# A hybrid attention block on one core: another order of the filler work, preloaded gate weights, byte masks, and a margin in the planner

## The chip, the core and the metric

The kernel runs on one core of a Trainium2 chip. A core has five engines that work side by side, each through its own queue in order: TensorE (PE, matrix products into PSUM), VectorE (DVE), ScalarE (ACT), GpSimd (POOL) and SyncE (SP), which here issues nearly all DMA transfers. The metric is the device time of one execution in microseconds (us); lower is better.

## What is computed

One layer of a hybrid decoder block over 1024 positions and 16 meta tokens in front of them, width 1024, float32. One projection feeds two branches: differential attention (8 heads) and gated linear attention, GLA (4 heads).

```python
u = rms_norm(h, norm_w); proj = u @ w_in
(a_q, a_k, a_v, a_z, g_q, g_k, g_v, g_z, g_lr, gate_a, gate_b) = jnp.split(proj, ...)
q1, q2 = partial_rope(qa[0], pos), partial_rope(qa[1], pos)   # the first 16 of 64 dims are turned
k1, k2 = partial_rope(ka[0], pos), partial_rope(ka[1], pos)
o_a = diff_attention(q1, q2, k1, k2, va, pos, lam)   # softmax(q1 k1) - lam softmax(q2 k2), times v
y_a = (norm(o_a) * silu(a_z)) @ w_branch_a
gk = (g_lr @ gla_gate_w2 + gla_gate_b)
lg = (jax.nn.log_sigmoid(gk) / GLA_GATE_NORMALIZER)
o_b = rms_norm(gla(qb, kb, vb, lg), gla_norm_w)      # chunked scan with decays exp(cumsum(lg))
y_b = (o_b * silu(g_z)) @ w_branch_b
merged = jax.nn.sigmoid(gate_a) * y_a + jax.nn.sigmoid(gate_b) * y_b
return h + merged @ w_out                            # then a final rms_norm; the meta tokens are dropped
```

## The kernel before

Every float32 product is made of three TensorE products of operands split into a high and a low part: `u_hi` with `w_hi`, `u_lo` with `w_hi`, `u_hi` with `w_lo`. ACT makes the high part, VectorE the low one. The kernel runs in stages:

- The front (0 to about 82 us) loads the x tiles, squares and scales them, transposes them on TensorE (L746) and projects the GLA keys.
- The projections (to about 591 us) are Strassen products (L563). They leave the gates in HBM (`d_g`, from tile `sg`, L295), and `ahead()` runs near their end: it loads, through POOL's queue, the first two weight tiles of the next stage.
- The GLA stage (about 592 to 880 us) runs 4 heads in two halves each. A half makes its gates (`ps_g`, L1294; then `lg`, L1303, and scans), the decay of the meta tokens (`dm`, L1344 to L1364, transposed on TensorE by L1348), the state (`st`), and a ladder of levels: `xl` on POOL (L1434), ACT (L1475) and VectorE (L1439), then `ps_l` on TensorE (L1446), then a masked copy (L1450). At its end the output is scaled (`oc`, L1537), transposed (L1542), made into `ob` (L1547) and stored to `d_ob`.
- Beside the heads run the fillers: projections that TensorE can do at any time. `fillers()` lists them in their order. `plain` projects a tile of 128 key columns in three pieces of 346, 348 and 346 positions (24 matmuls each), and `put` evacuates a piece: ACT writes the high part (L1160), VectorE the low part (L1163), SP stores it to `d_k` or `d_q`. `rope` does the same for the two tiles whose positions are turned: ACT copies both tiles to `rr` (L1194), SP loads a cosine and a sine table to `cs` (L1211, L1212), VectorE turns them (four products L1223 and two sums L1225 for a piece), and `put` follows. The rotary key tiles use `rope(8, ...)`; `rope(0, d_q, ...)` does the queries, whose raw projection is read back from HBM.
- Differential attention (about 880 to 1236 us) begins with the scores `ps_s` (L1734), a maximum (L1763) and the softmax on ACT (`p`, L1775); the branch product of GLA, `ps_y`, is its filler. The out stage follows.

Within each stage the order is made by a planner when the program is built (class `Schedule`). An instruction is an `op` with an engine, an estimated duration, dependencies, a priority and the ring (a set of buffers) that it takes a place in. `enter` gives it the earliest time at which its inputs are there: the end of each dependency plus a latency (`LAT`, or `SAME` on the same engine; 2.2 us after a DMA on SP). `run` then takes, engine by engine, the instruction that can start first; those that can start within `AHEAD` of each other go by priority. The result is a fixed order on each engine. On the chip, a semaphore wait holds its engine's whole queue.

Pieces of keys go to ring `qks`, two places which are the key tiles `kk0` and `kk1` of the later attention; `rr` and `cs` have one place each, the query tiles `q0` and `q1`. `PREP` is the time that the planner allows for the first operations of the GLA stage. The gate weights `w2r` (128 partitions, 16 rows of weights and a row of bias in groups of 32) are put together by a POOL memset and six DMAs (L1088 to L1092), and turned into `w2p` and `w2h` by ACT (L1093, L1095) and VectorE (L1096). The level masks come as float32 (`maskr`, L1099) and are cast to bytes on VectorE (L1100).

Of the kernel before, what the change touches and what calls it, by code (L numbers as in the profile page):

```python
# [77 lines left out]
class Schedule:  # L78
# [24 lines left out]
    def run(self):  # L103
# [60 lines left out]
def tile_hybrid_block(  # L164
# [11 lines left out]
    gate_b,  # L176
# [484 lines left out]
    with ExitStack() as es:  # L661
# [15 lines left out]
        def x_tile(i):  # L677
# [25 lines left out]
            ld = op("SP", 1.46 if n == P else 0.3, load, take="xt", lat=2.2, prio=pr)  # L703
# [118 lines left out]
        def keep(dst, lo_t, scale):  # L822
            def evac(_, o, y, ps, t0, n):
                v = {}

                def copy():
                    v["t"] = fe0.tile([P, 512], F32, name="stg", tag="st", bufs=2)[:, :n]
                    act(v["t"], ps(), AF.Copy, scale=scale)

                a = op("ACT", n / 1400 + 0.11, copy, (o,), take="st", use=(y,), prio=-1)  # L830
                op("SP", n / 700, lambda: nc.sync.dma_start(dst[:, t0 - lo_t : t0 - lo_t + n], v["t"]), (a,),
                   use=(("st", a),), lat=2.2, prio=-1)

            return evac
# [167 lines left out]
        b = op("SP", 3.0, begin, rest, lat=2.2, prio=200)  # L1002
# [6 lines left out]
    first = []  # L1009

    def ahead():

        for i in range(2):
            raw = wp["pool"].tile([P, KC * P], F32, name="w_raw", tag="w_raw", bufs=wp["nr"])
            nc.gpsimd.dma_start(raw, w_col[8 + i] if NV else w_row[4, i])
# [4 lines left out]
            first.append(hl)  # L1020

# [8 lines left out]
    def da_v(jobs, g, pre=None):  # L1030
# [3 lines left out]
        def evac(ti, o, y, ps):  # L1034
# [20 lines left out]
            stores.append(op("SP", 0.72, store, (b,), use=(("vs", a),), lat=2.2, prio=-1))  # L1055
# [16 lines left out]
    with ExitStack() as es:  # L1072
# [80 lines left out]
        def put(base, dst, i, raw, use, deps, c, n, t=None):  # L1153
# [16 lines left out]
            a = op("ACT", n / 1400 + 0.11, hi, deps, take="" if t else "qks", use=use, prio=-1)  # L1170
            b = op("DVE+" if t else "DVE", n / 960 + 0.07, lo, (a,), use=use, prio=-1)
            own = t.own if t else ("qks", a)
            qk_ops.append(op("SP", n / 350, store, (b,), use=(own,), lat=2.2, prio=-1))

        kn = [0]
# [6 lines left out]
        def plain(base, dst, i, pieces, lo_t):  # L1182
            w = jobs.weights(w_col[base + i])
            jobs.cols([w], pieces,
                      lambda _, o, y, ps, t0, n: put(base, dst, i, ps, (y,), (o,), slice(t0 - lo_t, t0 - lo_t + n), n))
# [88 lines left out]
        def gla_head(h):  # L1274
# [95 lines left out]
            def half_ops(hf, st):  # L1370
# [209 lines left out]
                for vh in range(2):  # L1580
# [4 lines left out]
                    op("SP", 1.46, lambda vh=vh: obs(vh), (c,), use=(("ob", b), ("oh", a)), lat=2.2, prio=-1)  # L1585
# [7 lines left out]
        def fillers():  # L1593
# [69 lines left out]
    with ExitStack() as es:  # L1663
# [19 lines left out]
        def load_k(h):  # L1683
# [4 lines left out]
            loads["k", h] = op("SP", 3.0 if h > 1 else 0.0, run if h > 1 else lambda: None, take="kk", lat=2.2, prio=16 * h)  # L1688

        def load_q(h, hf):  # L1690
# [4 lines left out]
            loads["q", h, hf] = op("SP", 3.0 if h else 0.0, run if h else lambda: None, take=f"q{hf}", lat=2.2,  # L1695
                                   prio=16 * h + 8 * hf)

        def load_v(h):
            for i, (k, us) in enumerate((("va", 1.5), ("vb", 1.5), ("vm", 0.5))):
                run = (lambda i=i: load_vp(h, i)) if h else lambda: None  # L1700
                st = tuple(vst[h // 2]) if h // 2 >= VA else ()
                loads[k, h] = op("SP", us if h else 0.0, run, st, take=k, lat=2.2, prio=16 * h + (8 if i == 1 else 4))
# [242 lines left out]
        def value(n):  # L1945
# [27 lines left out]
            z = op("SP", 0.5, lambda: load_z(n), (pv,), take="za", lat=2.2, prio=t0)  # L1973
# [27 lines left out]
        def o_load(kind, src, k, prio, deps, cs=(0,)):  # L2001
# [8 lines left out]
            for c in cs:  # L2010
                ops.append(op("SP", 3.0 / len(cs), lambda c=c: run(c), deps[c] + tuple(ops), take="" if c else f"o{k}", lat=2.2,
# [194 lines left out]
        def w_load(kk, late, i, r, deps):  # L2206
# [18 lines left out]
            return op("SP", 1.5 if i == 0 or not late else 0.75, run, deps, take="" if place else "raw" if late else f"wr{i}", lat=2.2, prio=LP)  # L2225

        for kk in range(4):
# [17 lines left out]
            def store(name, kk=kk, t=t, ops=ops):  # L2245
# [3 lines left out]
                stored[name, kk] = op("SP", 0.75, run, (ops[name],), use=(("x4", ops[name]),), lat=2.2, prio=-1)  # L2249
# [37 lines left out]
        def out_pair(p):  # L2287
# [84 lines left out]
            def x_load(i, c):  # L2372
# [6 lines left out]
                ld[i, c] = op("SP", 0.75, run, (s4op,) + d, take="x4" if i == c else "g4", prio=1500 + p, lat=2.2)  # L2379
# [110 lines left out]
def _consts():  # L2490
# [6 lines left out]
    m = np.zeros((P, len(LEVELS), P), f)  # L2497
# [17 lines left out]
def _layout(i):  # L2515
# [4 lines left out]
    hj = lambda m: m.reshape(D, HJ, 8, 8).transpose(0, 2, 1, 3).reshape(D, 1024)  # L2520
    cols = lambda m: m.reshape(KC, P, -1, P).transpose(2, 1, 0, 3)
# [11 lines left out]
        "gate_w2": a["gla_gate_w2"][0],  # L2533
        "gate_b": a["gla_gate_b"],
# [26 lines left out]
```

## Time and profile before

| | |
|---|---|
| median of 3 runs | 1393.76 us (1391.72 to 1394.04) |
| profiled execution | 1394.19 us, its span 1392.4 us |
| TensorE busy | 1332.8 us, 96% of the span |
| VectorE, ScalarE, GpSimd busy | 872.6, 749.0 and 580.9 us |
| mean granted TensorE clock | 0.992 of full speed |

Busy time is the time in which an engine executes, queued waits not counted. An idle time in brackets stands before the instruction that ended it, with what released it. The granted clock is a mean over a stretch; TensorE's two levels are 1.2 and 2.4 GHz, so 0.5 and 1.0.

### The profile page before, as it was taken

The numbers are of one execution on the slowest core, as the hardware profiler recorded it, in microseconds if no ns is written. First come the engines' busy times: TensorE is split into PE (matmuls) and PEld (weight loads), VectorE is DVE, ScalarE is ACT, GpSimd is POOL, SyncE is SP. The second block draws the span as 40 slices with busy tenths as digits, with TensorE's granted clock in tenths as the row PEclk, the third lists the DMA queues.
The fourth block names the chain that finished last, engine by engine and source line by source line (L and its number), as shares of the span: only waits on it lengthen the run. The fifth ranks groups of instructions, "written<-read, shape, count | busy, mean of one in ns | idle before, by whom it ended". The sixth has DMA issues, their size and how long they took to land. (4 is left out here: it accounts for less than half of the span.)

```text
span 1392.4 us, 22201 instructions
## 1 busy us (share of the span) xinstructions
PE 1332.8 (96%) x7736; PEld 1160.0 (83%) x7736; DVE 872.6 (63%) x1457; ACT 749.0 (54%) x1639; POOL 580.9 (42%) x598
## 2 busy tenths in 40 slices
PE   6999999999999999988999989799999999999998
PEld 5988889899888888788998989688888788778776
DVE  4845464555655444447676867487867778557775
ACT  7543332553656656544655454487777777422343
POOL 3113242442444232213463436256575665334444
PEclk9999999999999999999999999999999999999999
DMA  6216373324333333385524473588866555588332
GB/s 218 88 65 204 130 248 120 102 84 137 123 114 121 105 104 116 114 266 154 186 83 151 137 262 114 194 261 266 293 204 204 171 198 155 182 315 273 127 119 86
DMA packets 133747, 229.49 MB, mean 165 GB/s; under 512 B 14322, under 2 KB 60594, under 8 KB 133636
## 3 DMA queue, kind: packets, MB, share of 16 engines
q1 hardware_dynamic: 133348, 227.03, 49.7%
q8 instruction: 61, 1.00, 0.3%
q0 software_dynamic: 288, 1.05, 0.3%
q14 instruction: 50, 0.41, 0.1%
HBM read 143.81 MB, written 84.21 MB: 164 GB/s over the span
## 5 line engine op out<-in xcount | busy, mean ns | idle before, releaser
L511 POOL TENSOR_TENSOR s<-w_raw 128x512 f32<-128x512 f32 x48 | 69.9, 1475 | 194.5 <-DMA w_raw<-in_w_col_dram 133.1
L563 PE MATMUL ps_st<-th,wh 128*128 128x512 f32 x352 | 137.0, 389 | 0.2 <-DVE u L577 0.2
L563 PE MATMUL ps_st<-th,wl 128*128 128x512 f32 x352 | 136.9, 389 | 0.0
L563 PE MATMUL ps_st<-tl,wh 128*128 128x512 f32 x352 | 136.9, 389 | 0.0
L1434 POOL TENSOR_TENSOR xl<-lg 128x256 f32<-128x256 f32 x112 | 78.8, 728 | 93.5 <-PE ps_l L1446 36.8
L246 DVE TENSOR_TENSOR wl<-s,wh 128x512 fp32r<-128x512 f32 x96 | 77.0, 802 | 63.9 <-ACT wh L245 63.9
L245 ACT CAST wh<-s 128x512 fp32r<-128x512 f32 x96 | 59.4, 619 | 102.7 <-PE ps_st L563 56.0
L1775 ACT ACTIVATE p<-ps_s,nm 128x272 f32<-128x272 f32 (+7 forms) x128 | 96.6, 757 | 27.7 <-DVE nm L1763 18.2
L1763 DVE TENSOR_REDUCE nm<-ps_s 128x1 f32<-128x272 f32 (+7 forms) x128 | 97.1, 767 | 21.9 <-PE ps_s L1737 18.5
L426 PE MATMUL ps_proj<-u_hi,w_hi 128*128 128x346 f32 (+3 forms) x320 | 105.5, 330 | 4.7 <-ACT rr L1194 2.2
L563 PE MATMUL ps_st<-u_hi,wh 128*128 128x512 f32 x264 | 102.8, 389 | 1.0 <-issue 1.0
L563 PE MATMUL ps_st<-u_lo,wh 128*128 128x512 f32 x264 | 102.7, 389 | 0.0
L563 PE MATMUL ps_st<-u_hi,wl 128*128 128x512 f32 x264 | 102.7, 389 | 0.0
L427 PE MATMUL ps_proj<-u_lo,w_hi 128*128 128x346 f32 (+3 forms) x320 | 99.7, 312 | 1.3 <-DVE u_lo L755 1.3
L428 PE MATMUL ps_proj<-u_hi,w_lo 128*128 128x346 f32 (+3 forms) x320 | 99.2, 310 | 0.0
L245 ACT CAST wh<-w_raw 128x512 fp32r<-128x512 f32 x70 | 43.1, 616 | 93.5 <-PE ps_st L563 87.9
L246 DVE TENSOR_TENSOR wl<-w_raw,wh 128x512 fp32r<-128x512 f32 x70 | 61.2, 874 | 46.7 <-ACT wh L245 46.7
L563 PEld LDWEIGHTS ps_st<-th,wh 128*128 128x128 f32 x352 | 66.1, 188 | 14.3 <-ACT sg L289 0.6
L1734 PE MATMUL ps_s<-kk,q 128*128 128x264 f32 (+7 forms) x208 | 74.4, 362 | 3.7 <-ACT p L1775 3.6
L563 PEld LDWEIGHTS ps_st<-th,wl 128*128 128x128 f32 x352 | 66.1, 188 | 13.7
L563 PEld LDWEIGHTS ps_st<-tl,wh 128*128 128x128 f32 x352 | 66.1, 188 | 13.7
L511 POOL TENSOR_TENSOR s<-w_raw,s 128x512 f32<-128x512 f32 x22 | 28.5, 1295 | 115.3 <-DVE wl L246 115.3
(401 smaller groups left out, 4307.9 us busy)
## 6 DMA issues: line engine op xcount, KB each, us to landing
w_raw<-in_w_col_dram SPq DMA_DIRECT2D x54, 512.0 KB, 3.7
q<-d_q SPq DMA_DIRECT2D x32, 512.0 KB, 5.3
kk<-d_k SPq DMA_DIRECT2D x16, 520.0 KB, 7.0
d_g<-sg SPq DMA_DIRECT2D x32, 256.0 KB, 2.0
va<-d_v SPq DMA_DIRECT2D x16, 512.0 KB, 5.2
d_q<-qhi SPq DMA_DIRECT2D x24, 256.0 KB, 3.0
d_q<-qlo SPq DMA_DIRECT2D x24, 256.0 KB, 3.4
w_raw<-in_w_row_dram SPq DMA_DIRECT2D x12, 512.0 KB, 3.8
```

Of the source, the lines that this page charges most:

```text
L245: nc.scalar.copy(hi, raw)
L246: (eng or nc.vector).tensor_tensor(lo, raw, hi.bitcast(F32), ALU.subtract)
L426: mm(b["ps"], wh, rh, start=kc == 0, stop=False)
L427: mm(b["ps"], wh, rl, start=False, stop=False)
L428: mm(b["ps"], wl, rh, start=False, stop=kc == KC - 1)
L511: nc.gpsimd.tensor_tensor(r, x, y, op)
L563: mm(ps, w[:, k], x[k], start=start and k == 0 and i == 0, stop=k == KC // 2 - 1 and i == 2, skip_group_check=not start,)
L1434: nc.gpsimd.tensor_tensor(ap(X["xl", li], o1, *to), x if e else ref, ref if e else x, ALU.subtract)
L1734: mm(pp, qh, kk[:, c0 : c0 + w], start=True, stop=False)
L1763: nc.vector.tensor_reduce(b, ps, AX.XY if len(ps.shape) == 3 else AX.X, ALU.max, negate=True)
L1775: act(dst, ps, AF.Exp, bias=b, accum_out=stat[t]["sm"][:, j : j + 1])
```

## The change

- `fillers()`: the plain key tiles 2 and 3 come first, the rotary key tiles third. `ahead()` preloads the weights of those two plain tiles instead of the rotary ones.
- The gate weights are laid out on the host as one array of 128 rows; `ahead()` loads it with one DMA on POOL's queue, into a place of the weight ring. The memset and the six DMAs go.
- The masks are bytes in HBM and are loaded as such; the float32 tile and its cast go.
- Pieces of plain key tiles take their places in turn from `qks`, `qks`, `rr` and `cs`, so from four tiles instead of two.
- The planner: `PREP` is 7 instead of 11; the latency after a DMA is 3.0 instead of 2.2; an instruction on TensorE is taken to be ready 0.5 us (`MARGIN`) after its inputs from other engines. This holds in all stages.

```diff
-PREP = 11.0
-LAT = {"PE": 0.2, "ACT": 0.2, "DVE": 0.2, "POOL": 0.2, "SP": 2.2}
-SAME = {"PE": 0.0, "ACT": 0.13, "DVE": 0.13, "POOL": 0.13, "SP": 2.2}
+PREP = 7.0
+LAT = {"PE": 0.2, "ACT": 0.2, "DVE": 0.2, "POOL": 0.2, "SP": 3.0}
+SAME = {"PE": 0.0, "ACT": 0.13, "DVE": 0.13, "POOL": 0.13, "SP": 3.0}
+MARGIN = 0.5
...
         def enter(o):
-            o.at = max([d.end + (SAME[d.eng] if d.eng == o.eng else d.lat) for d in o.deps], default=0.0)
+            m = MARGIN if o.eng == "PE" else 0.0
+            o.at = max([d.end + (SAME[d.eng] if d.eng == o.eng else d.lat + m) for d in o.deps], default=0.0)
...
-            nc.gpsimd.dma_start(raw, w_col[8 + i] if NV else w_row[4, i])
+            nc.gpsimd.dma_start(raw, w_col[10 + i] if NV else w_row[4, i])
...
+        w2r.append(wp["pool"].tile([P, KC * P], F32, name="w2r", tag="w_hi", bufs=wp["nb"])[:, :512])
+        nc.gpsimd.dma_start(w2r[0], gate_w2)
...
-        w2r = s2.tile([P, 512], F32, name="w2r", tag="gq", bufs=3)
-        nc.gpsimd.memset(w2r, 0.0)
-        for i in range(4):
-            nc.sync.dma_start(w2r[32 * i : 32 * i + 16], gate_w2)
-            if i % 2 == 0:
-                nc.sync.dma_start(w2r[32 * i + 16 : 32 * i + 17], gate_b)
...
-        maskr = s2.tile([P, len(LEVELS), P], F32, name="maskr", tag="gk", bufs=2)
-        nc.sync.dma_start(maskr, c_masks)
-        nc.vector.tensor_copy(masks, maskr)
+        nc.sync.dma_start(masks, c_masks)
...
+            ring = "qks"
+            if not t:
+                ring = ("qks", "qks", "rr", "cs")[pn[0] % 4]
+                pn[0] += 1
+
             def hi():
-                v["t"] = t() if t else qks()
+                v["t"] = t() if t else qks() if ring == "qks" else sq.tile(
+                    [P, 2, 512], F32R, name="qks", tag={"rr": "q0", "cs": "q1"}[ring])
...
-            rope(8, d_k, KP, 0, first if NV else (None, None))
-            plain(8, d_k, 2, KP, 0)
+            for i in (2, 3):
+                plain(8, d_k, i, KP, 0, first[i - 2] if NV else None)
+            rope(8, d_k, KP, 0)
             if not NV:
                 gla_v(1)
-            for i in (3, 4, 5):
+            for i in (4, 5):
                 plain(8, d_k, i, KP, 0)
```

On VectorE, at the start of the GLA stage, this is the order before: the gate weights, the masks, the first turned piece and then the first gate.

```order
411 L1096 TENSOR_TENSOR w2p<-w2r,w2h 64x512
412 L1100 CAST masks<-maskr 128x1024
413 L1223 TENSOR_TENSOR qks<-rr,cs 128x346 x4
414 L1225 TENSOR_TENSOR qks<-qks 128x346 x2
415 L1163 SCALAR_TENSOR_TENSOR qks<-qks 128x346
416 L393 TENSOR_TENSOR w_lo<-w_raw,w_hi 128x512
417 L1163 SCALAR_TENSOR_TENSOR qks<-qks 128x346
418 L1303 SCALAR_TENSOR_TENSOR lg<-ps_g,lgt 128x16
```

And after the change:

```order
410 L1094 TENSOR_TENSOR w2p<-w2r,w2h 64x512
411 L1166 SCALAR_TENSOR_TENSOR qks<-ps_proj,qks 128x346
412 L1166 SCALAR_TENSOR_TENSOR qks<-ps_proj,qks 128x348
413 L1306 SCALAR_TENSOR_TENSOR lg<-ps_g,lgt 128x16
414 L1326 SCALAR_TENSOR_TENSOR lg<-ones,lg 128x16
415 L1347 TENSOR_TENSOR dm<-lg 128x16
416 L1306 SCALAR_TENSOR_TENSOR lg<-ps_g,lgt 128x512
417 L1367 TENSOR_TENSOR dm<-dm,gk 128x16
```

The turns have left this place, and `dm` follows the first gate at once. Their first row now is 482, among the levels of head 0 and behind its first outputs:

```order
481 L1453 COPY_PREDICATED mx_5655<-masks,ps_l 128x256 x3
482 L1226 TENSOR_TENSOR qks<-rr,cs 128x348 x4
483 L1228 TENSOR_TENSOR qks<-qks 128x348 x2
484 L1550 SCALAR_TENSOR_TENSOR ob<-ps_t,glaw,gz 128x512
485 L1166 SCALAR_TENSOR_TENSOR qks<-qks 128x348 x2
```

On SP at the start of the stage the last gate store (`d_g`) stood ahead of the masks before:

```order
136 L1090 DMA w2r<-in_gate_w_dram 16x512
137 L1092 DMA w2r<-in_gate_b_dram 1x512
138 L1090 DMA w2r<-in_gate_w_dram 16x512
139 L295 DMA d_g<-sg 128x512
140 L1090 DMA w2r<-in_gate_w_dram 16x512
141 L1092 DMA w2r<-in_gate_b_dram 1x512
142 L1090 DMA w2r<-in_gate_w_dram 16x512
143 L1099 DMA maskr<-in_c_masks_dram 128x1024
```

After the change it stands behind them:

```order
136 L1096 DMA masks<-in_c_masks_dram 128x1024
137 L1098 DMA ones<-in_c_ones_dram 128x128
138 L1100 DMA tri<-in_c_tri_dram 128x256
139 L1259 DMA gk<-d_gk 128x16
140 L1254 DMA gk<-d_gk 128x2x128
141 L296 DMA d_g<-sg 128x512
142 L1254 DMA gk<-d_gk 128x2x128 x3
```

The six loads of the gate weights are gone, and the gate store is now the sixth issue of the stage. On TensorE, the transpose of `dm` stands at row 3233 before, behind two gates (`ps_g`) and 189 filler matmuls of the stage, and at row 3115 after, behind 72. At the end of the GLA stage its last eight transposes and the first branch products stood next to each other before:

```order
4427 L453 MATMUL ps_proj<-w_hi,u_lo 128x256
4428 L454 MATMUL ps_proj<-w_lo,u_hi 128x256
4429 L1542 MATMUL ps_t<-ident,oc 128x128 x8
4430 L447 MATMUL ps_y<-w_hi,u_hi 48x256
4431 L448 MATMUL ps_y<-w_lo,u_hi 48x256
```

After the change the eight are two groups with 9 filler matmuls between them, and 30 of the kind that begins here stand behind the second group, before the first `ps_y` at row 4434:

```order
4401 L454 MATMUL ps_proj<-w_hi,u_lo 128x256
4402 L455 MATMUL ps_proj<-w_lo,u_hi 128x256
4403 L1545 MATMUL ps_t<-ident,oc 128x128 x4
4404 L453 MATMUL ps_proj<-w_hi,u_hi 128x256
4405 L454 MATMUL ps_proj<-w_hi,u_lo 128x256
4406 L455 MATMUL ps_proj<-w_lo,u_hi 128x256
```

Fillers have moved from earlier in the stage to its end.

## Rows read from the trace of the kernel before

**Rows 1.** The page: span, and busy time, share and instructions of each engine.
```profile
span 1392.4 us, 22201 instructions
PE 1332.8 (96%) x7736; PEld 1160.0 (83%) x7736; DVE 872.6 (63%) x1457; ACT 749.0 (54%) x1639; POOL 580.9 (42%) x598
```

**Rows 2.** Windows by stage: width, busy us of each engine, granted clock, DMA share, GB/s.
```profile
0.00:50.00 50.00, 35.47 (x248) 33.09 (x249) 30.76 (x56) 34.77 (x65) 14.44 (x25) 1.00 0.49 163
592.00:660.00 68.00, 59.09 (x342) 56.16 (x343) 43.96 (x96) 31.00 (x70) 17.08 (x23) 0.92 0.71 215
660.00:800.00 140.00, 136.23 (x930) 128.16 (x930) 103.04 (x214) 76.82 (x194) 66.67 (x80) 1.00 0.45 137
800.00:880.00 80.00, 72.61 (x521) 67.26 (x520) 52.55 (x109) 40.59 (x106) 33.21 (x39) 0.98 0.54 173
880.00:905.00 25.00, 19.17 (x122) 16.78 (x123) 12.31 (x25) 10.85 (x30) 9.20 (x14) 0.86 0.72 246
905.00:1236.00 331.00, 324.21 (x2076) 273.90 (x2075) 236.37 (x420) 230.15 (x608) 191.72 (x235) 1.00 0.67 221
```

**Rows 3.** Timeline of PE, GLA start: start, duration, instruction, idle before and releaser.
```profile
609.63 0.50 PE L1294 MATMUL ps_g<-glp,w2p 128*128 128x512 f32 x1 [1.80 <-DVE lg L1303]
620.85 0.43 PE L426 MATMUL ps_proj<-u_hi,w_hi 128*128 128x346 f32 x1 [2.24 <-ACT rr L1194]
633.21 0.38 PE L1348 MATMUL ps_t<-ident,dm 128*16 128x128 f32 x1 [3.36 <-DVE dm L1364]
```

**Rows 4.** Timeline of DVE at the GLA start: turns, gate, dm.
```profile
604.03 1.81 DVE L1223 TENSOR_TENSOR qks<-rr,cs 128x346 f32<-128x346 f32 x4 [1.02 <-DMA cs<-in_c_sin_dram]
...
616.41 0.52 DVE L1223 TENSOR_TENSOR qks<-rr,cs 128x348 f32<-128x348 f32 x1 [4.20 <-DMA d_k<-qks]
...
619.85 0.68 DVE L1303 SCALAR_TENSOR_TENSOR lg<-ps_g,lgt 128x512 f32<-128x512 f32 x1
...
627.68 0.52 DVE L1223 TENSOR_TENSOR qks<-rr,cs 128x346 f32<-128x346 f32 x1 [2.34 <-DMA d_k<-qks]
...
632.99 0.17 DVE L1364 TENSOR_TENSOR dm<-dm,gk 128x16 f32<-128x16 f32 x1
```

**Rows 5.** Timeline of ACT: the first evacuation of the GLA stage.
```profile
599.73 0.45 ACT L1194 COPY rr<-ps_proj 128x346 f32<-128x346 f32 x1 [3.82 <-DMA d_g<-sg]
```

**Rows 6.** Timeline of SP's queue: last gate store and masks.
```profile
595.94 0.35 SPq L295 DMA_DIRECT2D d_g<-sg  x1
...
598.81 0.35 SPq L1099 DMA_DIRECT2D maskr<-in_c_masks_dram  x1
```

**Rows 7.** Timelines of ACT and PE, 811 to 817 us.
```profile
811.91 1.23 ACT L1160 ACTIVATE qks<-qks 128x512 fp32r<-128x512 f32 x2 [3.15 <-DVE qks L1225]
...
814.69 0.33 PE L1542 MATMUL ps_t<-ident,oc 128*128 128x128 f32 x1 [2.29 <-ACT oc L1537]
815.85 1.21 PE L1542 MATMUL ps_t<-ident,oc 128*128 128x128 f32 x3 [0.83 <-ACT oc L1537]
```

**Rows 8.** Timeline of POOL; then L1439 by line: ns min/median/max.
```profile
623.23 4.35 POOL L1434 TENSOR_TENSOR xl<-lg 128x256 f32<-128x256 f32 x6 [31.30 <-DVE lg L1334]
...
L1439 DVE TENSOR_TENSOR xl<-xl,gq x56: 406/418/1524, 635.3 to 865.3; 128x256 f32<-128x256 f32 x56
```

**Rows 9.** Timeline of PE at the switch to differential attention.
```profile
879.89 0.66 PE L1542 MATMUL ps_t<-ident,oc 128*128 128x128 f32 x4 [1.05 <-DVE ob L1547]
881.54 0.42 PE L447 MATMUL ps_y<-w_hi,u_hi 128*48 128x256 f32 x1 [0.99 <-DVE ob L1547]
...
886.03 0.39 PE L452 MATMUL ps_y<-w_hi,u_hi 128*128 128x256 f32 x1 [0.39 <-DVE vraw L1043]
...
890.43 0.39 PE L1734 MATMUL ps_s<-kk,q 128*128 128x272 f32 x1 [3.08 <-ACT p L1775]
```

**Rows 10.** Timelines of SP's queue and ACT in the front: the second pair of x tiles.
```profile
26.01 0.88 SPq L683 DMA_DIRECT2D xt<-in_x_dram  x2
...
32.34 1.06 ACT L691 ACTIVATE sq<-xt 128x1024 bf16<-128x1024 f32 x1 [2.31 <-DMA xt<-in_x_dram]
```

More of the change, by code (lines that the diff above doesn't have):

```diff
@@ L702, in x_tile @@
             pr = XP[i]
-            ld = op("SP", 1.46 if n == P else 0.3, load, take="xt", lat=2.2, prio=pr)
+            ld = op("SP", 1.46 if n == P else 0.3, load, take="xt", lat=3.0, prio=pr)
             s = op("ACT", 1.04, square, (ld,), use=(("xt", ld),), prio=pr)
@@ L1007, in tile_hybrid_block @@
                 o.run()
-    first = []
+    first, w2r = [], []
     def ahead():
@@ L1054, in evac @@
             b = op("DVE", 0.34, lo, (a,), use=(y,), prio=-1)
-            stores.append(op("SP", 0.72, store, (b,), use=(("vs", a),), lat=2.2, prio=-1))
+            stores.append(op("SP", 0.72, store, (b,), use=(("vs", a),), lat=3.0, prio=-1))
         stores = []
@@ L1168, in store @@
                         nc.sync.dma_start(d[:, 8 * i : 8 * i + 8, c], v["t"][:, e, :n].bitcast(F32))
-            a = op("ACT", n / 1400 + 0.11, hi, deps, take="" if t else "qks", use=use, prio=-1)
+            a = op("ACT", n / 1400 + 0.11, hi, deps, take="" if t else ring, use=use, prio=-1)
             b = op("DVE+" if t else "DVE", n / 960 + 0.07, lo, (a,), use=use, prio=-1)
-            own = t.own if t else ("qks", a)
-            qk_ops.append(op("SP", n / 350, store, (b,), use=(own,), lat=2.2, prio=-1))
-        kn = [0]
+            own = t.own if t else (ring, a)
+            qk_ops.append(op("SP", n / 350, store, (b,), use=(own,), lat=3.0, prio=-1))
+        kn, pn = [0], [0]
         def qks():
@@ L1180, in qks, with plain @@
             return t[:, :1024].rearrange("p (e n) -> p e n", e=2)
-        def plain(base, dst, i, pieces, lo_t):
-            w = jobs.weights(w_col[base + i])
+        def plain(base, dst, i, pieces, lo_t, pre=None):
+            w = jobs.weights(w_col[base + i], pre=pre)
             jobs.cols([w], pieces,
@@ L1686, in run @@
                     load_kj(A["pool"] if h % 2 else sq, h, j)
-            loads["k", h] = op("SP", 3.0 if h > 1 else 0.0, run if h > 1 else lambda: None, take="kk", lat=2.2, prio=16 * h)
+            loads["k", h] = op("SP", 3.0 if h > 1 else 0.0, run if h > 1 else lambda: None, take="kk", lat=3.0, prio=16 * h)
         def load_q(h, hf):
@@ L1693, in run @@
                     load_qj(A["pool"] if hf else sq, h, hf, j)
-            loads["q", h, hf] = op("SP", 3.0 if h else 0.0, run if h else lambda: None, take=f"q{hf}", lat=2.2,
+            loads["q", h, hf] = op("SP", 3.0 if h else 0.0, run if h else lambda: None, take=f"q{hf}", lat=3.0,
                                    prio=16 * h + 8 * hf)
@@ L1701, in load_v @@
                 st = tuple(vst[h // 2]) if h // 2 >= VA else ()
-                loads[k, h] = op("SP", us if h else 0.0, run, st, take=k, lat=2.2, prio=16 * h + (8 if i == 1 else 4))
+                loads[k, h] = op("SP", us if h else 0.0, run, st, take=k, lat=3.0, prio=16 * h + (8 if i == 1 else 4))
         S_, M_, E_, FB_, A_ = {}, {}, {}, {}, {}
@@ L2223, in run @@
                     nc.sync.dma_start(r[i].rearrange("p (a n) -> p a n", a=2), d_t[kk].rearrange("a p n -> p a n"))
-            return op("SP", 1.5 if i == 0 or not late else 0.75, run, deps, take="" if place else "raw" if late else f"wr{i}", lat=2.2, prio=LP)
+            return op("SP", 1.5 if i == 0 or not late else 0.75, run, deps, take="" if place else "raw" if late else f"wr{i}", lat=3.0, prio=LP)
         for kk in range(4):
@@ L2378, in x_load @@
                 d += xl[-2:]
-                ld[i, c] = op("SP", 0.75, run, (s4op,) + d, take="x4" if i == c else "g4", prio=1500 + p, lat=2.2)
+                ld[i, c] = op("SP", 0.75, run, (s4op,) + d, take="x4" if i == c else "g4", prio=1500 + p, lat=3.0)
                 xl_.append(ld[i, c])
@@ L2532, in _layout @@
         "subln_w": a["da_subln_w"].reshape(P, 1),
-        "gate_w2": a["gla_gate_w2"][0],
-        "gate_b": a["gla_gate_b"],
+        "gate_w2": np.concatenate(
+            [v for i in range(4) for v in (a["gla_gate_w2"][0], a["gla_gate_b"] if i % 2 == 0 else z[:1], z[:15])]
+        ),
         "gla_w": a["gla_norm_w"][0].reshape(2, P).T,
```

22 lines of the change are left out of this document (11 added, 11 removed).

## The prediction, made before the changed kernel was run

> **What bounds the kernel now.** I read the page's busy shares first. TensorE is busy 1332.8 us of a span of 1392.4, and no other engine comes near [rows 1]. The change leaves every product in place, so only two things can move the time: the 59.6 us in which TensorE stands idle, and the stretches in which it works at the lower clock. I therefore read the table of windows next [rows 2]; width less PE busy gives the idle time of each stage, and (1 - granted clock) x PE busy estimates what the clock costs there:
>
> - front, 0 to 50: 14.5 us idle, full clock.
> - start of the GLA stage, 592 to 660: 8.9 idle, clock 0.92, so 0.08 x 59.1 = 4.7 lost.
> - middle, 660 to 800: 3.8 idle of 140, full clock.
> - late GLA, 800 to 880: 7.4 idle, clock 0.98, 1.5 lost.
> - the switch to differential attention, 880 to 905: 5.8 idle, clock 0.86, 0.14 x 19.2 = 2.7 lost.
> - differential attention, 905 to 1236: 6.8 idle of 331.
>
> Then I read the single waits. At the GLA start three are long: 1.80, 2.24 and 3.36 us, 7.4 together [rows 3]. VectorE's rows say why [rows 4]. Its queue is in order, and there it turns the rotary key tiles (L1223). Each turn waits for something slow: 1.02 for the sine table, 4.20 and 2.34 for key stores, which must land before one of the two places for key pieces is free. Behind the turn at 616.41 stands the second gate (L1303, 619.85); behind that at 627.68 stands dm (L1364, 632.99), for which TensorE waits 3.36. The filler matmuls in front of those points have run out by then. The clock falls to its 1.2 GHz level around these waits, which is the 4.7 us.
>
> **The change, part by part.** The profiled run takes 1394.2 us, 0.4 above the median of the runs; the sum is made against it.
>
> *Lists at the GLA start.* Two plain key tiles now lead, and the rotary tile follows third. The order shows VectorE going from w2p straight to two lower halves of plain pieces and then to lg and dm, with no turn before them; the first turn stands far behind the first levels of head 0. On TensorE dm's transpose stands behind 72 filler matmuls instead of 189. With 59.1 us for 342 matmuls, 0.17 each [rows 2], head 0 begins about 20 us of TensorE work earlier. So the three waits (7.4) and their clock (4.7) lose their cause: 12.1 gross. What is late next, each bounded:
> (a) The first evacuation. The first copy waited until 599.73, 3.82 us, for the last gate store to land [rows 5]. That store was issued at 595.94, before the masks at 598.81 [rows 6]; now masks, ones, tri and two key loads are issued ahead of it, and the two ACT casts for w2p stand before the last sigmoid. The evacuation gets later rather than earlier. Two PSUM places and 45 fillers cover some of it; I put 1.5 us (0 to 3.5, the upper end being a second wait like rows 5's).
> (b) The levels of head 0 take the place of bare fillers for 20 us. At the rate of the middle, 3.8 of 140, that is 0.5 (0 to 1.5).
> (c) The rotary turns did not go away; they now stand among head 0's levels, and their table loads wait in SP's queue behind gq and gv loads. What that can do is in the trace once: at 811.91 ACT waits 3.15 us for a rotary turn, oc (L1537) is queued behind it, and TensorE waits 2.29 and 0.83 [rows 7]. With the clock's 1.5 us it cost 4.6. Three turned pieces are moved; I take half of one such event, 2.5 (0 to 14, three of them), since four places for pieces, two of them the rotary ones, let the stores drain earlier.
> The gain here is 12.1 - 4.5 = 7.6 us (-6 to 12).
>
> One rule speaks against (c). In the rows, the POOL products of a head (L1434) begin at 623.23, after most turns; L1439 takes 418 ns in the median and up to 1524 beside them [rows 8]. The turns' 18 instructions (12 of L1223, 6 of L1225) could so grow a little, hidden under a VectorE that is 63% busy [rows 1]. The Trainium skill, "SBUF — State Buffer", section "Who interferes with whom", states that a VectorE instruction with two SBUF inputs contends with a GpSimd instruction that reads SBUF, and that the second to issue blocks fully. By that rule each of the 18 could wait out one POOL product, 4.35 / 6 = 0.73 us, 13 us of VectorE in all; the median here shows no such block, the maximum one. Neither enters the sum.
>
> *Gate weights and masks.* Six SP issues, the POOL memset and the 0.69 us cast on VectorE go, and the masks shrink from 512 to 128 KB. None of these is what a TensorE wait ends on: the w2p product at the first gate had long been made, and VectorE then waited 1.02 for the sine table [rows 4]. I take nothing. The cover is that the new load is issued on POOL inside the projections, where TensorE has no wait to speak of; if it landed late, the first gate would wait for it, at most some 3 us, inside the bounds of (a).
>
> *Rest of the GLA stage.* There are 3.8 + 7.4 us idle and 1.5 of clock; the last wait before the switch is counted below. The margin puts TensorE instructions 0.5 us later than before behind their ACT or VectorE producers, which is larger than most of the short gaps; the event at 811.91 may vanish or turn up again, as the turns of q stand elsewhere. Fillers moved to the end leave other places barer. I take +1.5 (-5 to +6).
>
> *The switch.* The last transposes (L1542) were followed at once by the y products: 1.05 and 0.99 us for ob, 0.39, then 3.08 for the first softmax [rows 9], with the lower clock after them. The order now puts 9 fillers between the two last groups of transposes and 30 after them; at 0.15 us each (136.2 us for 930 matmuls [rows 2]) the 30 cover 4.4 us. The waits of 1.05, 0.99 and 0.39 should go, with most of the 2.7 of clock; the 3.08 stays, because only six y products stand before the first scores. That is 2.4 + 2.1 = 4.5 (0 to 8).
>
> *Front.* The second pair of x tiles was issued at 26.01, behind a store, and the square waited 2.31 for it [rows 10]; now four loads stand together. Most of the 14.5 idle lies before that and stays. I take +1.5 (-1 to 2.5).
>
> *Differential attention.* 6.8 us in gaps all below 1 us, of the size the margin is about; the order is reshuffled throughout. +0.5 (-4 to +4). The out stage barely moves: 0 (±1).
>
> Sum: 7.6 + 1.5 + 4.5 + 1.5 + 0.5 = 15.6. 1394.2 - 15.6 = 1378.6, and 0.4 less as a median: **1378**.
>
> **Rivals.**
> *The wait only moves.* The first evacuation waits for the late gate store and its shortage of PSUM places keeps TensorE idle (3.5), two rotary turns hold head 0 (9.2). Then the GLA start gives 12.1 - 3.5 - 0.5 - 9.2, about -1, and only the front and the switch are left, 6.0: about 1389. For it: the d_g landing ended the first wait [rows 5], the event of rows 7. Against it: four places for pieces, and the event of rows 7 came once in the whole stage. 0.16.
> *Slower.* One mechanism: a rotary turn standing in VectorE's order among the levels, waiting for its table or its place. If it waits longer than the fillers in front of the next level last, which is about 2 us where 12 stand there (12 x 0.17), TensorE stops and the clock falls after it. Three key pieces and the two of q at 4.6 each are 23, with (a) at 3.5 and (b) at 0.5 it is 27 against 12.1 + 6.0 gained: 1394 + 9, about 1403. For it: VectorE has waited 4.20 and 2.34 for exactly such landings [rows 4]. Against it: those came with two places and the table load directly ahead of its use. 0.13.
> *The lists do nothing.* The planner's times are not the chip's; a new order removes some gaps and makes as many elsewhere, within 1391 to 1396.5. For it: TensorE is at 96% already. Against it: the three waits have a cause that is gone. 0.11.
> *Forecast*, 1367 to 1386: 0.60.
>
> **How the numbers follow.** Bounds taken as independent, the sum can miss by about 10 us to either side. The range 1366 to 1392 holds the forecast and the moved wait and leaves out the slower end and part of "nothing", about 2 in 10. A measurement of this kernel can tell 0.2%, 2.8 us. Faster: 0.60 + 0.16 + 0.02 = 0.78; within: 0.09; slower: 0.13.
>
> **What would show it.** Right: in the windows 592 to 660 idle below 6 us and a clock above 0.97, VectorE's first L1223 turn after head 0's first levels, no PE wait on dm above 1 us; at the switch no wait on ob, and the softmax wait of about 3 us still there. Wrong: a PE wait of over 2 us on a level or on oc with a rotary turn or its table ahead of it in VectorE's rows, or a first evacuation after 602. If differential attention moves by more than 4 us to either side, the margin did more there than I could read.

## The result: 1.4% faster, and where it came from

The changed kernel takes 1373.13 us in the median (1372.48 to 1377.55), the kernel before 1393.9; the ratio is 0.9861 with an interval of 0.9838 to 0.9884. The gain is 20.8 us; 15.6 were forecast, and the range held it. The head of the page after answers to [rows 1]:

```profile
span 1370.7 us, 22183 instructions
PE 1320.3 (96%) x7736; PEld 1153.7 (84%) x7736; DVE 875.6 (64%) x1456; ACT 748.7 (55%) x1639; POOL 591.0 (43%) x598
```

A way to compare two lists with the same products is to cut both traces at the same landmarks of the work: first Strassen product, first key product of the GLA stage, first branch product, first product of the other branch, first product of the out stage. Both kernels then have the same products between the landmarks (some 20 move over the one between the fourth and fifth part). The view is that of windows: width, busy us (and instructions) of PE, PEld, DVE, ACT, POOL, then granted clock, DMA share, GB/s. The kernel before:

```profile
0.00:83.20 83.20, 67.67 (x521) 65.05 (x521) 51.74 (x99) 50.82 (x101) 18.22 (x28) 1.00 0.40 133
83.20:590.80 507.60, 507.39 (x2584) 434.65 (x2584) 256.70 (x342) 253.87 (x428) 174.03 (x127) 1.00 0.39 129
590.80:881.50 290.70, 268.51 (x1793) 251.90 (x1792) 201.50 (x419) 150.07 (x371) 118.88 (x146) 0.98 0.53 165
881.50:971.10 89.60, 82.67 (x606) 74.06 (x607) 65.97 (x126) 62.42 (x172) 47.97 (x63) 0.96 0.77 257
971.10:1304.20 333.10, 327.46 (x1876) 270.41 (x1875) 234.93 (x378) 199.06 (x500) 179.53 (x204) 1.00 0.66 223
1304.20:1392.40 88.20, 79.13 (x361) 63.99 (x359) 61.75 (x95) 32.76 (x71) 42.26 (x33) 0.99 0.26 90
```

The changed kernel:

```profile
0.00:79.80 79.80, 65.99 (x521) 63.83 (x521) 52.45 (x99) 50.81 (x101) 18.21 (x28) 0.98 0.41 139
79.80:587.90 508.10, 507.41 (x2584) 434.75 (x2584) 255.19 (x342) 253.40 (x427) 174.45 (x128) 1.00 0.39 129
587.90:857.50 269.60, 258.54 (x1793) 246.43 (x1793) 204.16 (x418) 150.72 (x373) 123.27 (x145) 1.00 0.56 176
857.50:944.40 86.90, 79.21 (x585) 70.65 (x586) 64.26 (x122) 59.91 (x165) 45.05 (x57) 0.98 0.80 262
944.40:1278.70 334.30, 328.81 (x1899) 272.94 (x1897) 237.88 (x381) 201.42 (x506) 187.24 (x210) 1.00 0.66 223
1278.70:1370.70 92.00, 80.33 (x361) 65.09 (x359) 61.62 (x96) 32.47 (x71) 42.83 (x33) 0.96 0.25 86
```

Width by width: front 3.4 us shorter, projections 0.5 longer, GLA stage 21.1 shorter, the start of differential attention 2.7 shorter, its rest 1.2 longer, the out stage 3.8 longer; together 21.7, the difference of the spans. In sum the GLA stage is the whole gain: its idle time fell from 22.2 to 11.1 us, and its PE busy time by 10.0. The clock (0.98 to 1.00) makes an estimated 0.02 x 268.5 = 5.4 of the 10.0; the rest is not traced to a cause here. The parts four and five hold the same products only together: together they are 1.5 us shorter.

Its first part answers to [rows 2]:

```profile
592.00:660.00 68.00, 65.32 (x413) 62.31 (x412) 54.29 (x109) 37.01 (x87) 26.44 (x32) 1.00 0.67 208
660.00:800.00 140.00, 136.54 (x953) 129.86 (x952) 108.86 (x227) 80.94 (x209) 67.56 (x79) 1.00 0.53 166
```

2.7 us are idle where 8.9 were, and the clock is 1.00 where it was 0.92. The waits of 1.80, 2.24 and 3.36 us [rows 3] have no successor of more than 0.9: in the timeline of PE these are the two longest of that part (start, duration, instruction, idle before and releaser).

```profile
599.21 0.43 PE L427 MATMUL ps_proj<-u_hi,w_hi 128*128 128x346 f32 x1 [0.70 <-DVE qks L1166]
...
636.58 0.68 PE L1449 MATMUL ps_l<-xl 128*128 128x128 f32 x4 [0.89 <-DVE xl L1442]
```

At the switch, PE's rows answer to [rows 9]: the waits of 1.05 and 0.99 us for ob are gone, two of 0.96 and 0.90 for other evacuations stand in their place, and the softmax wait is 1.69 instead of 3.08.

```profile
857.46 0.32 PE L448 MATMUL ps_y<-w_hi,u_hi 128*48 128x256 f32 x1 [0.96 <-DVE vs L1051]
860.44 0.38 PE L453 MATMUL ps_y<-w_hi,u_hi 128*128 128x256 f32 x1 [0.90 <-DVE vraw L1047]
864.78 0.45 PE L1738 MATMUL ps_s<-kk,q 128*128 128x272 f32 x1 [1.69 <-ACT p L1779]
```

The windows on both sides of the first branch product, from 800 us to it and 25 us behind it, first the kernel before:

```profile
800.00:881.50 81.50, 73.16 (x524) 67.57 (x522) 53.30 (x110) 41.08 (x106) 34.09 (x40) 0.98 0.54 173
881.50:906.50 25.00, 20.12 (x129) 17.82 (x129) 12.95 (x27) 11.82 (x35) 9.11 (x16) 0.86 0.74 259
```

The changed kernel:

```profile
800.00:857.50 57.50, 54.88 (x422) 52.47 (x420) 38.76 (x81) 28.84 (x71) 28.70 (x33) 1.00 0.52 169
857.50:882.50 25.00, 21.99 (x152) 19.67 (x153) 15.77 (x31) 14.65 (x40) 9.66 (x15) 0.93 0.81 271
```

From 800 us to the end of the GLA stage 2.6 us are idle instead of 8.3; in the 25 us behind it 3.0 instead of 4.9.

### The profile page after: what moved, and what is told of

Same layout as the page of the kernel before. It is cut to its first block, busy times and chain, and to the rows that moved or that the text cites. A ratio compares the mean times of both kernels' runs of the same rounds, so it can differ in the third digit from the quotient of the medians.

```text
span 1370.7 us, 22183 instructions
## 1 busy us (share of the span) xinstructions
PE 1320.3 (96%) x7736; PEld 1153.7 (84%) x7736; DVE 875.6 (64%) x1456; ACT 748.7 (55%) x1639; POOL 591.0 (43%) x598
## 4 chain that ended last, share of the span: by engine, by line
PE 78%; DVE 8%; ACT 4%; DMA 4%; issue 3%; POOL 2%; SPq 0%; POOLq 0%; DVEq 0%; ACTq 0%
PE ps_st L564 28%; PE ps_st L589 6%; PE ps_proj L427 3%; PE ps_proj L428 3%; PE ps_proj L429 3%; PE ps_t L2361 2%; PE ps_s L2021 2%; PE ps_s L2022 2%; PE ps_s L2023 2%; PE ps_s L1738 2%; PE ps_l L1449 2%; PE ps_t L1852 2%; PE ps_s L1739 1%; PE ps_y L2021 1%; PE ps_y L2361 1%
## 5 line engine op out<-in xcount | busy, mean ns | idle before, releaser
L246 ACT CAST wh<-w_raw 128x512 fp32r<-128x512 f32 x70 | 43.1, 616 | 94.0 <-PE ps_st L564 88.5
```

Of the source, the lines that this page charges most:

```text
L246: nc.scalar.copy(hi, raw)
```

## The experiments

My reading gave the gain at the GLA start to the order of the fillers (theory O). The rival gave it to the planner's numbers (theory P). Each kernel's ratio is against the kernel before, timed beside it on the same chip; the last two columns are widths from each run's profiled execution, cut as above. A width of the same list varies by up to about 1 us from run to run: the front, with the planner's old numbers, took 83.2 us in the kernel before and 82.2 in two runs of the table.

| kernel | median us | ratio (interval) | GLA stage | out stage |
|---|---|---|---|---|
| before | 1392.2 to 1393.9 | 1 | 290.7 | 88.2 |
| changed | 1373.13 | 0.9861 (0.9838 to 0.9884) | 269.6 | 92.0 |
| plain first alone | 1398.67 | 1.0047 (1.0030 to 1.0064) | 295.4 | 87.9 |
| planner's numbers alone | 1381.26 | 0.9922 (0.9907 to 0.9936) | 279.0 | 91.8 |
| changed, rotary first | 1377.83 | 0.9897 (0.9878 to 0.9916) | 278.2 | 92.0 |
| changed, two places | 1376.29 | 0.9892 (0.9871 to 0.9913) | 275.2 | 92.0 |
| changed, old planner | 1395.02 | 1.0015 (0.9998 to 1.0032) | 290.4 | 89.9 |
| margin alone | 1384.70 | 0.9947 (0.9932 to 0.9962) | 284.4 | 87.8 |
| changed, no margin | 1383.75 | 0.9940 (0.9925 to 0.9955) | 280.6 | 92.6 |
| changed, old last list | 1368.45 | 0.9830 (0.9814 to 0.9846) | 269.3 | 88.3 |
| changed, old gate load and masks | 1373.26 | 0.9865 (0.9841 to 0.9888) | 270.6 | 91.7 |
| old last list, margin 1.0 | 1380.70 | 0.9918 (0.9897 to 0.9939) | 278.1 | 88.5 |
| changed, PREP 11 | 1378.01 | 0.9895 (0.9874 to 0.9916) | 274.1 | 90.3 |
| changed, 2.2 us after a DMA | 1375.27 | 0.9874 (0.9852 to 0.9895) | 278.3 | 88.8 |

### Plain tiles first, alone

```diff
-            nc.gpsimd.dma_start(raw, w_col[8 + i] if NV else w_row[4, i])
+            nc.gpsimd.dma_start(raw, w_col[10 + i] if NV else w_row[4, i])
...
-            rope(8, d_k, KP, 0, first if NV else (None, None))
-            plain(8, d_k, 2, KP, 0)
+            for i in (2, 3):
+                plain(8, d_k, i, KP, 0, first[i - 2] if NV else None)
+            rope(8, d_k, KP, 0)
```

> The kernel before with one edit: the plain key tiles 2 and 3 lead the fillers with their weights preloaded, the rotary tile is third; the planner's numbers, the two places, the gate weights and the masks stay as before. On TensorE the decay's transpose stands behind 144 filler matmuls (192 with the gates before, 75 in the changed kernel). Theory O (order: the rotary turns at the head of VectorE's row are what TensorE waits for at the GLA start): the first 68 us of the GLA stage lose their 8.9 us idle down to about 3 and their clock rises from 0.92 to 1.0, so about 10 us are gained, 1384 us. Theory P (planner: the numbers move the heads forward and the margin covers the waits, the order of the fillers alone does little): within 3 us of before, 1391 to 1394.

Neither held: it is 0.5% slower. The start of its GLA stage has a new wait, and three timelines tell it. ACT is idle for 9.74 us ahead of the third evacuation, and what ends it is the landing of the store of the first piece:

```profile
611.54 0.46 ACT L1160 ACTIVATE qks<-ps_proj 128x346 fp32r<-128x346 f32 x1 [9.74 <-DMA d_k<-qks]
```

That store was issued on SP only at 605.48, behind the loads of the first head:

```profile
604.55 0.89 SPq L1251 DMA_DIRECT2D gq<-d_gq  x2
605.48 1.17 SPq L1168 DMA_DIRECT2D d_k<-qks  x2
```

The first gate's evacuation stands behind it on ACT, and TensorE waits for the gate:

```profile
614.10 0.80 PE L1294 MATMUL ps_g<-glp,w2p 128*128 128x512 f32 x1 [5.81 <-DVE lg L1303]
```

With two places, a plain piece at the head does what the rotary turn did: something slow stands ahead of the gate in an in-order queue. Later in the stage more is lost: from 800 us on TensorE waits 4.8 us for xl, before 1.6.

### The planner's numbers, alone and with four places

```diff
-PREP = 11.0
+PREP = 7.0
-LAT = {"PE": 0.2, "ACT": 0.2, "DVE": 0.2, "POOL": 0.2, "SP": 2.2}
+LAT = {"PE": 0.2, "ACT": 0.2, "DVE": 0.2, "POOL": 0.2, "SP": 3.0}
+MARGIN = 0.5
```

> The kernel before with only the planner's numbers of the change: PREP 7, 3.0 us after a DMA, 0.5 us of margin; the rotary tile still leads, two places, old gate weights and masks. VectorE's row begins with the turns again; dm's transpose stands behind 150 rows of the stage on TensorE, and 72 fillers stand at the end before the branch products. Theory O: the three long waits of the GLA start are still there in some form, so only the late part of the stage and the switch gain, about 9 us: 1385. Theory P: nearly all of the gain, 1373 to 1377.

This alone makes half of the gain. The turns still head VectorE's row and TensorE still waits 2.21 us for the rr copy at 618.37, but the GLA stage is 11.7 us shorter. Theory P fell short as well: 8 us of the gain are missing.

The changed kernel with the rotary tile first again:

```diff
-            for i in (2, 3):
-                plain(8, d_k, i, KP, 0, first[i - 2] if NV else None)
-            rope(8, d_k, KP, 0)
+            rope(8, d_k, KP, 0, first if NV else (None, None))
+            for i in (2, 3):
+                plain(8, d_k, i, KP, 0)
```

> The changed kernel with the rotary tile leading again and its weights preloaded; four places, preloaded gate weights, byte masks and the planner's numbers as changed. TensorE's order is that of the planner's numbers alone. Theory O: about 10 us above the changed kernel, 1383, with waits of TensorE on dm or on the evacuation in the first 68 us of the GLA stage. Theory P: within 3 us of the changed kernel, 1370 to 1376. Against the run with the planner's numbers alone it shows what four places and the gate load give: nothing beyond 2 us by both theories.

It lies between the two expectations: 4.7 us above the changed kernel in the medians (the intervals just overlap), 8.6 in the GLA stage. Its profiled execution was the slowest of its four, so the width is rather too large. Against the planner's numbers alone the stage differs by 0.8 us, so four places and the gate load give little while the turns lead (the medians differ by 3.4 us, with intervals that overlap).

### Two places in the changed kernel

```diff
-                ring = ("qks", "qks", "rr", "cs")[pn[0] % 4]
+                ring = "qks"
```

> The changed kernel with two places for key pieces instead of four; all else as changed. Theory O: the turns stand late either way and plain pieces need a place only from evacuation to the landing of their stores, some 4 us of the 3.9 us that a piece takes on TensorE, so within 3 us of the changed kernel, 1371 to 1376. Rival R (the places carry the gain): the third piece waits for the store of the first, ACT and with it the gates behind it are held, TensorE waits 2 to 4 us at several pieces: 1378 or more.

The time lies between the two expectations. Rival R's mechanism is there, at one piece: ACT waits 5.09 us for the landing of a key store, kmt is queued behind it, and TensorE waits 4.18.

```profile
608.25 0.46 ACT L1163 ACTIVATE qks<-ps_proj 128x346 fp32r<-128x346 f32 x1 [5.09 <-DMA d_k<-qks]
```

```profile
609.42 1.21 PE L1359 MATMUL ps_d<-gvm,kmt 16*128 16x256 f32 x2 [4.18 <-ACT kmt L1355]
```

The GLA stage is 5.6 us longer. The medians differ by 3.2 with overlapping intervals, so the size is uncertain; the wait is not.

### All of the change but the planner's numbers

```diff
-PREP = 7.0
+PREP = 11.0
-LAT = {"PE": 0.2, "ACT": 0.2, "DVE": 0.2, "POOL": 0.2, "SP": 3.0}
+LAT = {"PE": 0.2, "ACT": 0.2, "DVE": 0.2, "POOL": 0.2, "SP": 2.2}
-MARGIN = 0.5
+MARGIN = 0.0
```

> The changed kernel with all of the planner's old numbers (PREP 11, 2.2 us after a DMA, no margin): plain tiles lead, four places, preloaded gate weights, byte masks. The run with plain tiles first and two places was slower than before: its third piece waited 9.74 us on ACT for the store of the first, which stood on SP behind twelve loads. Theory Q (the order helps only where that piece has a place of its own): with four places the wait is gone, the GLA stage goes from 295.4 us (plain first, two places) to about 283, 1383 to 1386 in all, and planner and order then add up to the whole gain. Rival (the order is worth nothing, the planner is all): the stage stays above 290, 1392 or more.

This run decided most. In the time and in the stage the rival's numbers held. The start is as clean as theory Q wanted, but the stage as a whole gains nothing. Its windows:

```profile
592.00:660.00 68.00, 64.22 (x402) 60.85 (x403) 49.41 (x102) 36.61 (x86) 23.79 (x31) 1.00 0.69 206
660.00:800.00 140.00, 133.82 (x912) 125.75 (x911) 104.04 (x211) 72.34 (x182) 61.57 (x74) 0.98 0.53 164
800.00:880.00 80.00, 69.87 (x482) 63.66 (x480) 48.23 (x103) 37.95 (x102) 33.80 (x39) 0.95 0.43 137
```

By [rows 2], the first part has 3.8 us idle instead of 8.9 and no loss of clock; the second 6.2 instead of 3.8, clock 0.98; the third 10.1 instead of 7.4, clock 0.95 instead of 0.98. What was won at the start is given back before the end: TensorE does 60 products more in the first part than before and 57 fewer in the other two. So the change without the planner's numbers gives nothing, these numbers alone 0.8%, and both together 1.4%. One of the places is the mechanism that I had put down as the slower rival. A turn of q on VectorE waits 3.41 us for its loads (the reload of rr was issued at 784.28, directly ahead of gz):

```profile
791.63 2.50 DVE L1226 TENSOR_TENSOR qks<-rr,cs 128x512 f32<-128x512 f32 x4 [3.41 <-DMA gz<-d_gz]
```

```profile
784.28 1.20 SPq L1207 DMA_DIRECT2D rr<-d_rq  x1
785.58 1.26 SPq L1384 DMA_DIRECT2D gz<-d_gz  x2
```

A level's xl is queued behind the turn, and TensorE waits for it, with the lower clock after that:

```profile
796.66 1.22 PE L1449 MATMUL ps_l<-xl 128*128 128x128 f32 x4 [3.38 <-DVE xl L1442]
```

### The margin: alone, left out, and doubled

```diff
+MARGIN = 0.5
...
-            o.at = max([d.end + (SAME[d.eng] if d.eng == o.eng else d.lat) for d in o.deps], default=0.0)
+            m = MARGIN if o.eng == "PE" else 0.0
+            o.at = max([d.end + (SAME[d.eng] if d.eng == o.eng else d.lat + m) for d in o.deps], default=0.0)
```

> The kernel before with the margin of 0.5 us on TensorE alone. 54 fillers then stand at the end of the GLA stage before the branch products (none before), dm's transpose behind 186 rows (192). Theory M (the margin is what the planner's numbers bring): nearly the gain of the three numbers together, 1380 to 1384, with the late waits on oc, on the last transposes and at the switch gone. Rival (PREP and the latency after a DMA bring it, by moving the heads forward): 1388 to 1393.

8.1 us, a little less than expected: the margin is the larger part of the planner's numbers, not all of it. The waits for oc [rows 7] and at the last transposes are gone; one of 3.02 for xl stands at 821.50.

The changed kernel with `MARGIN = 0.0`:

> The changed kernel without the margin; PREP 7, 3.0 us after a DMA, order, places, gate weights as changed. No filler stands between the last transposes and the branch products, as before. Theory M: the waits at the end of the stage and at the switch are back, the GLA stage takes 278 us or more instead of 269.6, 1381 to 1386. Rival: within 3 us of the changed kernel, 1371 to 1376.

As theory M wanted, in the time and in the place. The first part of the stage is clean without the margin (65.78 us busy of 68). The end of the stage has waits for ob again, of 0.85 and 0.90 where before had 1.05 and 0.99, and one of 2.93 for oc ahead of them:

```profile
867.19 1.42 PE L1545 MATMUL ps_t<-ident,oc 128*128 128x128 f32 x4 [2.93 <-ACT oc L1540]
869.46 1.11 PE L1545 MATMUL ps_t<-ident,oc 128*128 128x128 f32 x4 [0.85 <-DVE ob L1550]
871.47 0.45 PE L448 MATMUL ps_y<-w_hi,u_hi 128*48 128x256 f32 x1 [0.90 <-DVE ob L1550]
```

Doubled (`MARGIN = 1.0` in the first two lists, the old last list below):

> The fastest kernel so far (changed front and GLA lists, old numbers for the last list) with a margin of 1.0 us instead of 0.5 in the first two lists. If a margin works because it puts cover ahead of waits of its own size (theory M), more of it is as good or better: GLA stage 266 to 271 us, 1366 to 1370 in all. If what counts is which order the list happens to fall into (theory L: here no filler is left between the last transposes and the branch products, and dm stands behind 117 rows instead of 75), the stage is 276 us or longer: 1375 to 1383.

Theory L held here: the stage is 8.8 us longer than with 0.5, and the same waits stand at its end although the margin is larger than some of them:

```profile
863.16 1.42 PE L1545 MATMUL ps_t<-ident,oc 128*128 128x128 f32 x4 [2.06 <-ACT oc L1540]
865.43 0.68 PE L1545 MATMUL ps_t<-ident,oc 128*128 128x128 f32 x4 [0.85 <-DVE ob L1550]
867.01 0.45 PE L448 MATMUL ps_y<-w_hi,u_hi 128*48 128x256 f32 x1 [0.90 <-DVE ob L1550]
```

The windows from 800 us to the first branch product, with a margin of 0 and of 1.0:

```profile
800.00:871.50 71.50, 63.30 (x450) 57.42 (x448) 47.20 (x99) 37.36 (x99) 31.78 (x39) 0.98 0.45 141
...
800.00:867.00 67.00, 58.78 (x433) 54.30 (x433) 45.77 (x97) 33.21 (x85) 31.57 (x38) 0.99 0.51 167
```

Both have 8.2 us idle there, the changed kernel 2.6. So 0.5 us isn't a size that covers waits of 0.5 us. What the runs show is where the fillers end up. No filler stands between the last transposes and the branch products with margins of 0 and 1.0, 30 do in the changed kernel and 54 with the margin alone; the late waits are there in the first two and gone in the others. No run moves fillers there by hand, so that this place alone makes the difference is argued, not shown.

### The old last list

```diff
+        sch.margin = 0.0
+        LAT["SP"] = SAME["SP"] = 2.2
         op = sch.op
         n_of = lambda t: NM + P * (t % 8 + 1)
```

> The changed kernel with the planner's old numbers for the last list only (differential attention and the out stage), whose TensorE order is then that of the kernel before; front and GLA stage as changed. By the stages of the two profiled runs (from the first branch product on 510.9 us before, 513.2 changed, the out stage 88.2 against 92.0) it gains 2.3 us over the changed kernel: 1369 to 1372. Rival (the stages are not independent, or the out stage's loss comes from elsewhere): 1372.5 to 1376.

It came out at 1368.45 us, half a microsecond below the expected range: in the medians 4.7 less than the changed kernel, where 2.3 were expected (the intervals just overlap). GLA and out stage, by the windows:

```profile
587.50:856.80 269.30, 258.61 (x1793) 246.54 (x1793) 203.75 (x418) 149.81 (x372) 123.35 (x145) 1.00 0.56 176
...
1277.80:1366.10 88.30, 79.04 (x361) 63.98 (x359) 61.55 (x95) 32.66 (x71) 42.12 (x33) 0.99 0.27 90
```

The out stage has its 88 us back. In the changed kernel TensorE waits there 2.65, 1.1 and 0.9 us for VectorE; in the kernel before and in this run it waits 1.8 and 0.5. The longest wait, and the clock behind it:

```profile
1300.68 0.47 PE L2361 MATMUL ps_y<-u_hi 128*128 128x512 f32 x1 [2.65 <-DVE x L2463]
```

```profile
1302.00:1304.00 2.00, 2.00 (x6) 1.58 (x5) 0.20 (x2) 0.72 (x2) 1.16 (x2) 0.50 0.00 0
```

### Gate load, PREP, latency after a DMA

The memset, the six loads and the float32 masks back in the changed kernel:

```diff
-        nc.gpsimd.dma_start(w2r[0], gate_w2)
+        nc.gpsimd.memset(w2r, 0.0)
+        for i in range(4):
+            nc.sync.dma_start(w2r[32 * i : 32 * i + 16], gate_w2[:16])
...
+        nc.sync.dma_start(maskr, c_masks)
+        nc.vector.tensor_copy(masks, maskr)
```

> The changed kernel with the gate weights put together by a memset and six small loads at the start of the GLA stage and float32 masks cast on VectorE, as before; TensorE's order is unchanged to the last row. If the preload and the byte masks only take work off queues that nothing waits for (my prediction's step: no gain), it stays within 2 us of the changed kernel, 1371 to 1375. Rival: the second list now asks for w2p some 9 us earlier, the loads stand on SP ahead of the last gate store, and the first evacuation and gate wait for them: 2 to 6 us slower, 1375 to 1379, with the added waits before 605 us.

No difference (1373.26 against 1373.13). TensorE's only wait for w2p is 0.3 us.

`PREP = 11.0`:

> The changed kernel with PREP 11 instead of 7: dm's transpose stands behind 144 rows of the stage instead of 75, 30 fillers still at the end. If the start is what PREP serves, the first gate is asked for some 10 us later and the first head starts later, but fillers are there for TensorE: no long wait at the start, and the price is that fillers are used up early: GLA stage 272 to 277 us, 1375 to 1380. Rival: nothing, 1371 to 1375.

As expected in the time: 4.9 us slower in the medians (the intervals just overlap), the GLA stage 4.5 longer. Its start has one wait of 1.68; later two of 2.04 and 1.47 stand on xl.

2.2 us after a DMA in all lists:

> The changed kernel with 2.2 us after a DMA instead of 3.0 in all lists. In the rows a key store takes 2.7 to 7.0 us to land, so the larger number is nearer to the chip: with 2.2 the list puts turns and reloads before their data are there, and a wait of 2 us or more appears on TensorE behind a DMA or a turn: 1376 to 1382. Rival: the margin covers it, 1371 to 1376.

Not told apart from the changed kernel in time, as the rival said. The expected wait is there all the same: its GLA stage is 8.7 us longer, with 2.8 us on xl; what follows is 5.0 shorter up to the out stage, and that one 3.2 shorter. The latency's gain in one list is paid for in another.

## Why the prediction was right, and which steps were wrong

- **The GLA start** (7.6 us forecast). Idle 8.9 to 2.7 and the clock's 4.7 make 10.9. The three waits did lose their cause. Of what was to come next, (a) is there: the first evacuation is at 598.15, 8.0 us behind the first key product instead of 7.0, but TensorE waits only 0.70 for it. The profile puts ACT's wait down to a gate product; the gate store, issued at 595.62, landed 2.4 us later, at about the same moment. (c) cost 0.9 instead of 2.5. The lower bound of this sum is -7 by its own terms, not -6.
- **What failed is the step behind it.** I took what the start gains as gained for the run. With the old numbers a start as clean gives 10 us, and the rest of the stage takes them back; with plain tiles first and two places the start keeps a wait of 5.81. I had named four places as a help to the stores, not as the condition without which the order costs the stage 5 us.
- **Rest of the GLA stage** (+1.5, bounds -5 to +6) is the mis-sized term: 21.1 for the stage, less 10.9, less 1.1 counted with the switch, leaves 9.1, above the upper bound. From 660 us to the stage's end the idle time fell from 12.1 to 6.1. I had priced the margin by the length of single gaps; where it puts the fillers was in the order (30 before the branch products), but I used that for the switch alone.
- **Switch** (4.5 forecast). Ahead of the first branch product 2.0 us of waits for ob became 0.96 for another evacuation, 1.1 won; in the 25 us behind it 1.9 of idle time are won and, by the clock's 0.86 and 0.93, an estimated 1.3. That is 4.3, right in size; but new waits stand where I had expected none, and the one that I said would stay at 3.08 is 1.69.
- **Front**: 3.4 against 1.5 and an upper bound of 2.5. All four loads are issued at 20.91, and the second pair of squares no longer waits.
- **Gate weights and masks**: nothing, as forecast, by the run that puts them back.
- **Differential attention and out stage**: 0.5 (-4 to +4) and 0 (±1) forecast. The two parts behind the first branch product are 1.5 us shorter together; less the switch's 3.2, differential attention lost 1.7. The out stage lost 3.8. "Barely moves" was wrong: waits of 2.65, 1.1 and 0.9 us stand where 1.8 and 0.5 stood.
- **The rivals.** The moved wait came with two places. The slower one's mechanism came with the old planner's numbers at 3.4 us, and in a smaller size in the changed kernel too: the last turns of q wait 2.76 us on VectorE for their loads, and TensorE then waits 1.39 for a level queued behind them, without a loss of clock.

```profile
797.00 2.50 DVE L1226 TENSOR_TENSOR qks<-rr,cs 128x512 f32<-128x512 f32 x4 [2.76 <-DMA gz<-d_gz]
```

```profile
802.62 0.71 PE L1449 MATMUL ps_l<-xl 128*128 128x128 f32 x4 [1.39 <-DVE xl L1442]
```

The errors have both signs: 3.3, 7.6 and 1.9 too little at the start, in the rest of the stage and in the front, 6.0 too much in differential attention and the out stage. The total was nearer than its terms, and that is luck.

## What to carry to other kernels

A wait removed at the head of a stage is only a gain if the filler work that it used is put where the next wait stands; so price a changed order over the whole stage, and give one list's numbers to that list alone if another one loses by them. Before a load or a store is put behind others in an in-order queue, look at which place it frees and who stands behind the one that waits for it.

## What the runs showed of the hardware

The turns met POOL, as the one rule in the prediction said. In the changed kernel's DVE rows, the first four turns, of 346 columns, took 4.03 us, where the kernel before took 1.81 [rows 4], and the two sums right behind them took 0.94 (the mean of these sums is 512 ns in both kernels). These turns come first; the row 482 shown above as the first is the second piece, at 645.41.

```profile
630.01 4.03 DVE L1226 TENSOR_TENSOR qks<-rr,cs 128x346 f32<-128x346 f32 x4
633.97 0.94 DVE L1228 TENSOR_TENSOR qks<-qks 128x346 f32<-128x346 f32 x2
```

POOL's rows in that time run without a gap and end at 633.67:

```profile
630.35 1.57 POOL L1463 TENSOR_TENSOR at<-mx,tri 128x512 f32<-128x512 f32 x1
631.88 1.79 POOL L1437 TENSOR_TENSOR xl<-lg 128x256 f32<-128x256 f32 x2
```

TensorE's 0.89 us at 636.58 are the end of it: the level that it waits for is queued behind the turns. Over the stage the key turns' mean rose from 514 to 791 ns (346 columns, 8 of them) and from 516 to 753 (348, 4 of them), 3.2 us of VectorE, between the nothing of my sum and the 13 us of every instruction blocked. The out stage shows the same at a larger size: VectorE's split of 512 columns takes 0.68 us, and 1.78 beside a POOL instruction of 1.67 (L2326 at 1294.78, POOL's L2458 at 1294.33). The Trainium skill, "SBUF — State Buffer", section "Who interferes with whom", has the cause: a VectorE instruction with two SBUF inputs contends with a GpSimd instruction that reads SBUF, and the lock between them is exclusive. Both places agree with it.

I hadn't expected how long a store can take to free its place. In the plain-first run the first of a piece's two key stores was issued at 605.48, and ACT went on at 611.54, 6 us later, where the median key store of the kernel before (173 KB) lands in 2.7.
